# Wide exponentials behind one Silu, value products of two query blocks in one burst, and pre-multiplied last weights in a hybrid transformer block

## The chip, the cores and the metric

The kernel runs on one core of a Trainium2 chip. The metric is the time of one execution on the device in microseconds. In this text TensorE is PE (its weight loads PEld), VectorE is DVE, ScalarE is ACT, GpSimd is POOL, and SyncE, which starts most of the transfers, is SP.

## The reference

One block of a transformer, for one sequence of 1024 tokens of width 1024. A conditioning vector c gives six modulation vectors; attention (8 heads of 64 in three dilated branches) and a gated delta rule (8 heads of 64) run side by side on projections of the normed input; then come an output projection, a SwiGLU network of width 2816 and a last norm:

```python
sh1, sc1, g1, sh2, sc2, g2 = split(silu(c) @ w_ada + b_ada, 6)
h = rmsnorm(x, norm_attn_g) * (1 + sc1) + sh1
q_a, k_a, v_a, q_d, k_d, v_d, z_d, b_d, a_d = split(h @ w_in)
y_attn = dilated_attention(q_a, k_a, v_a, rel_bias)
# delta heads: q, k, v = silu(causal_conv(q_d, k_d, v_d)); q, k = l2norm(q) / 8, l2norm(k)
#   beta = sigmoid(b_d); g = -exp(a_log) * softplus(a_d + dt_bias); gcum = cumsum(g) in a chunk
#   decay[i, j] = exp(gcum[i] - gcum[j]) for j <= i; A = strict_lower((beta k) k^T * decay)
#   u, w = (I + A)^-1 [beta v, beta k exp(gcum)]; then a scan over the chunks carries the state
y_delta = rmsnorm(o, delta_norm_g) * silu(z_d)
x = x + g1 * (concat(y_attn, y_delta) @ w_out)
h = rmsnorm(x, norm_ffn_g) * (1 + sc2) + sh2
x = x + g2 * ((silu(h @ w_gate) * (h @ w_up)) @ w_down)
return rmsnorm(x, final_norm_g)
```

l2norm divides by the square root of the sum of squares plus 1e-6.

## The kernel before, in words

Every large product is made of three matmuls: both operands are split into a high part (a cast, for weights on ACT, line 230, or 1603 in the network) and a low part (a subtraction, on POOL, line 231, or on DVE, line 1604), and high*high, high*low and low*high are added in one PSUM bank. gemm (line 590) and proj_t (line 613) issue them for the projections, down_mm (line 1809) for the last product.

A scheduler orders the instructions of each engine once, when the program is built, by priority and by what they need; each engine then runs its queue in that order and waits at the first instruction whose inputs are not there. Three things steer it: urgent() raises the priority of what is issued within, issue_after(x) puts an instruction behind x, and a table FILL says how many microseconds of projections are put between two pieces of the delta or attention work (ahead, turn).

**The delta heads** are done in two groups g of four heads, as eight blocks n of 128 tokens. conv (lines 549 to 557) is the causal convolution, a scaled copy on ACT, three multiply-adds on DVE (line 553) and a Silu on ACT (line 557). delta_turn transposes a conv's output (line 734, tiles trk and trq), squares it on ACT (line 740) and sums the squares on DVE (line 744) into norms rk (keys) and eq (queries). For group 1 this is done early, by delta_early, which stores the convs' outputs in memory, from where delta(1) loads them again. delta_rows loads the rows of gcum into four tiles dt of 128x1024, one a head, and masks them. delta_prep makes from rk its inverse root by Ln and Exp (lines 761 to 763), subtracts Gc (line 764), and then takes decay * rk as 32 exponentials of 128x128 (line 767), each with its own bias column. kk (line 796) are the products of keys with keys and queries, multiplied with dt on DVE (line 802); the results go to memory (line 809). kt*kds (line 821) and qd*eb (line 836) are on POOL, where eb is one more exponential per pair of heads (line 835) of rows that are loaded just before.

delta_rows_in loads the stored rows again; delta_v (lines 872, 875) makes beta*v; delta_inverse scales by bpr (line 885), runs 31 steps on DVE, each needing the one before (lines 896, 900), writes the result tn to memory and loads it again (lines 903, 905); the products on TensorE that use it begin at line 928. delta_scan carries the state; it takes a power on POOL (line 1063). Meanwhile TensorE does projections as fill, among them va (values of attention) and z. z's output is evacuated by a Silu on ACT (line 634). Silu and Exp lie in different tables of ACT, so a change from one to the other is a table load.

**Attention** takes units of one pair of heads hp and one query block qb of 128 rows, 32 units. att_score (lines 1325 to 1336) makes scores S, adds the bias table and takes the maximum on DVE, the exponential on ACT and the scaling on POOL, into X. att_turn transposes X block by block (line 1349, tiles tr) and copies it to et (line 1354 on ACT for key blocks 0 to 3, line 1352 on DVE for 4 to 7); et has ETB buffers for the two heads of ETB/2 units. att_value multiplies et with va (line 1366), the two heads e side by side in the two halves of the array's columns, in qb+1 steps, into bank y. attend issues the value product of a unit AV = 3 units behind its scores.

**The last product** of the network is a scheme of seven products of half-size matrices, down(0) to down(6); each has 22 slices f of the inner dimension, four row blocks b, and three matmuls each. down_parts loads a slice of both operands and splits them. An "end" of a product adds up what it needs: half_end multiplies by g2 (g2r, line 1858), adds x (xr, line 1859) and squares with a sum (line 1861); row_out takes the root (line 1868), its reciprocal (line 1869), and scales both halves of the row block (line 1874 on ACT, line 1876 on DVE) and stores them. In down(6) the last TAIL = 4 slices are kept back: their matmuls come block by block, with each block's end behind it.

## Time and profile before

| | us |
|---|---|
| median of three runs | 1407.59 (1407.41 to 1409.31) |
| the profiled execution | 1407.41 |
| its span (first to last instruction) | 1405.6 |
| TensorE busy | 1353.3 |
| VectorE, ScalarE, GpSimd busy | 874.6, 660.0, 287.2 |

A row of the profile's groups reads: line, engine, operation, output<-input, shape and count, then the busy time of all, the mean nanoseconds of one, and the idle time of the engine just before them with what ended it. A row of the timeline reads: start, duration, engine, line, operation. A row of waits reads: engine and tile that waited, what it waited for, then the sum in us, how many times, and the longest. In a row of windows each engine's busy time and its instruction count follow the window's length; then come TensorE's granted clock (1.00 is full speed), the DMA share and GB/s. The chain of work that ended last goes back from the last instruction, at each step to what released it.

### The profile page before, as it was taken

What the parts mean: (1) busy time and instruction counts of PE and PEld (TensorE: products, weight loads), DVE (VectorE), ACT (ScalarE), POOL (GpSimd) and SP (SyncE); (2) the same over time, 40 slices, a digit from 0 to 9 for tenths busy, and PEclk for the clock granted to TensorE, in tenths of its full rate; (3) what the DMA queues carried; (4) which work ended last, traced back from release to release, by engine and by line L of the source; (5) the groups of instructions that cost most, each with busy time, mean ns of one, the idle gap of its engine ahead of it and who ended that gap; (6) DMA issues with size and microseconds to landing.
All of it is one profiled execution on the core that took longest, in us unless ns stands there. A gap on an engine that the chain in (4) does not pass through costs nothing.

```text
span 1405.6 us, 24430 instructions
## 1 busy us (share of the span) xinstructions
PE 1353.3 (96%) x8984; PEld 1113.2 (79%) x8984; DVE 874.6 (62%) x1659; ACT 660.0 (47%) x1285; POOL 287.2 (20%) x261
## 2 busy tenths in 40 slices
PE   8998999998999999999999899999999999999997
PEld 4777787888889878777777678888888888888885
DVE  3688573656847242765248987666575776474487
ACT  4497424346233453765168533333333333444456
POOL 2344303324213433543262400000000000000000
PEclk9999999999999999999999999999999999999999
DMA  8666573475362555521675245444453665765566
GB/s 305 225 194 174 173 217 127 135 233 140 120 171 85 173 146 166 158 84 61 198 251 161 97 163 180 157 164 164 137 195 113 209 209 182 255 223 195 195 225 232
DMA packets 169872, 245.65 MB, mean 175 GB/s; under 512 B 32566, under 2 KB 73831, under 8 KB 169752
## 3 DMA queue, kind: packets, MB, share of 16 engines
q1 hardware_dynamic: 169752, 244.08, 54.2%
q8 instruction: 71, 1.16, 0.3%
q14 instruction: 49, 0.40, 0.1%
HBM read 181.27 MB, written 67.48 MB: 177 GB/s over the span
## 4 chain that ended last, share of the span: by engine, by line
PE 71%; DVE 13%; DMA 6%; ACT 4%; issue 3%; POOL 1%; SPq 0%; DVEq 0%; ACTq 0%; POOLq 0%
PE wua L1614 8%; PE wga L1614 8%; PE X L1809 6%; PE g_a L590 4%; PE wuc L1614 4%; PE Z L1809 4%; PE wgc L1614 4%; PE wo L590 3%; PE y L1366 2%; PE Y L1809 2%; PE tr L1349 2%; PE g_va L613 2%; DVE tm L896 2%; PE f L251 2%; PE wgb L1614 2%
## 5 line engine op out<-in xcount | busy, mean ns | idle before, releaser
L1604 DVE TENSOR_TENSOR wl_db<-wr_db,wh_db 128x512 fp32r<-128x512 f32 x77 | 53.2, 690 | 75.7 <-ACT wh_db L1603 75.6
L1603 ACT CAST wh_db<-wr_db 128x512 fp32r<-128x512 f32 x77 | 47.9, 622 | 97.7 <-PE X L1809 41.3
L1329 DVE CUSTOM_DVE_ANT_0 X<-S,ng 128x512 f32<-128x512 f32 (+3 forms) x64 | 36.6, 587 | 61.9 <-PE S L1326 46.4
L1809 PE MATMUL X<-wl_db,wh_da 128*128 128x512 f32 x176 | 68.6, 390 | 0.1
L1336 POOL TENSOR_SCALAR X<-X,sc 128x128 f32<-128x128 f32 (+7 forms) x64 | 50.0, 786 | 91.1 <-DVE sc L1335 77.7
L1809 PE MATMUL X<-wh_db,wl_da 128*128 128x512 f32 x176 | 68.5, 389 | 0.0
L1809 PE MATMUL X<-wh_db,wh_da 128*128 128x512 f32 x176 | 68.5, 389 | 0.0
L1334 ACT ACTIVATE X<-X,sc 128x128 f32<-128x128 f32 (+7 forms) x64 | 49.4, 773 | 33.9 <-DVE sc L1329 31.7
L1604 DVE TENSOR_TENSOR wl_da<-wr_da,wh_da 128x512 fp32r<-128x512 f32 x77 | 52.8, 686 | 1.6 <-ACT wh_da L1603 1.6
L590 PE MATMUL wo<-yh,wh_wo 128*128 128x512 f32 x128 | 51.7, 405 | 1.0 <-DVE xo L1417 1.0
L590 PE MATMUL g_a<-hh,wh_a 128*128 128x512 f32 x128 | 51.8, 404 | 0.0
L590 PE MATMUL wo<-yh,wl_wo 128*128 128x512 f32 x128 | 50.8, 397 | 0.0
L590 PE MATMUL wo<-yl,wh_wo 128*128 128x512 f32 x128 | 50.4, 394 | 0.1
L1603 ACT CAST wh_da<-wr_da 128x512 fp32r<-128x512 f32 x77 | 47.4, 616 | 6.4 <-PE wua L1614 5.9
L590 PE MATMUL g_a<-hl,wh_a 128*128 128x512 f32 x128 | 50.3, 393 | 0.0
L590 PE MATMUL g_a<-hh,wl_a 128*128 128x512 f32 x128 | 50.1, 392 | 0.0
L1603 ACT CAST wh_wg_s<-wg_s 128x512 fp32r<-128x512 f32 x33 | 20.5, 622 | 55.8 <-PE wuc L1614 23.8
L1349 PE MATMUL tr<-ident,X 128*128 128x128 f32 x288 | 42.9, 276 | 1.8 <-ACT et L1354 1.0
L1366 PE MATMUL y<-et,va 128*64 128x128 f32 x576 | 43.9, 280 | 0.0
L231 POOL TENSOR_TENSOR wl_wo<-wr_wo,wh_wo 128x512 fp32r<-128x512 f32 x24 | 32.5, 1357 | 51.7 <-ACT wh_wo L230 51.7
L1603 ACT CAST wh_wg<-wr_wg 128x512 fp32r<-128x512 f32 x31 | 19.3, 621 | 47.2 <-PE wua L1614 19.2
L1603 ACT CAST wh_wu_s<-wu_s 128x512 fp32r<-128x512 f32 x33 | 20.4, 622 | 44.5 <-PE wga L1614 17.5
(545 smaller groups left out, 4349.9 us busy)
## 6 DMA issues: line engine op xcount, KB each, us to landing
wm<-in_wada SPq DMA_DIRECT2D x44, 512.0 KB, 6.0
wr_da<-ao_d SPq DMA_DIRECT2D x77, 256.0 KB, 3.0
wr_wu<-in_wu SPq DMA_DIRECT2D x50, 256.0 KB, 2.8
wr_wg<-in_wg SPq DMA_DIRECT2D x48, 256.0 KB, 3.0
ao_d<-a SPq DMA_DIRECT2D x44, 256.0 KB, 2.6
wr_wd<-in_wdn SPq DMA_DIRECT2D x44, 256.0 KB, 3.0
wr_db<-wt_d SPq DMA_DIRECT2D x44, 256.0 KB, 2.7
ao_d<-as SPq DMA_DIRECT2D x33, 256.0 KB, 2.5
```

Source lines behind the costliest of these rows:

```text
L231: (eng or nc.gpsimd).tensor_tensor(out=lo[:, :n], in0=raw[:, :n], in1=hi[:, :n].bitcast(F32), op=ALU.subtract)
L251: nc.tensor.matmul(first[bank], a[:, w0], b[k][:, cs], start=(k == 0 and n_ == 0), stop=(k == KT - 1 and n_ == 2))
L590: last[0] = nc.tensor.matmul(ps, a[:, w0], b[k0 + k4][:, cs], start=(i == 0), stop=(i == n - 1))
L1329: nc.vector.tensor_tensor_reduce(out=X[:, c0:c1], in0=ps[:, 0 : c1 - c0], in1=ng[:, u + c0 : u + c1], scale=1.0, scalar=(3e38 if m is None ...
L1334: nc.scalar.activation(X[:, 0:nk], X[:, 0:nk], AF.Exp, scale=-1.0, bias=m, accum_out=sc[:, 2:3])
L1336: nc.gpsimd.tensor_scalar(out=X[:, 0:nk], in0=X[:, 0:nk], scalar1=sc[:, 3:4], scalar2=0.0, op0=ALU.mult, op1=ALU.add)
L1349: nc.tensor.transpose(ps[:, (kb - c0) * P : (kb - c0 + 1) * P], X[:, kb * P : kb * P + P], ident)
L1366: nc.tensor.matmul(yps[64 * e : 64 * e + 64, yc], va[:, kb, 64 * e : 64 * e + 64], ets[e][:, kb, :], start=(kb == 0), stop=(kb == qb),)
L1603: nc.scalar.copy(hi, src)
L1604: (eng or nc.vector).tensor_tensor(out=lo, in0=src, in1=hi.bitcast(F32), op=ALU.subtract)
L1614: nc.tensor.matmul(ps, a[:, w0], b, start=(first and k == 0 and n_ == 0), stop=(k == 3 and n_ == 2), skip_group_check=True,)
L1809: nc.tensor.matmul(bank[b], a[:, ts_], w, start=(first and f == 0 and n_ == 0), stop=(f == NF - 1 and n_ == 2), skip_group_check=True,)
```

## The change

It has three parts.

**Group 1 of the delta heads.** delta_rows(1) also subtracts Gc from each dt on DVE, so that the exponential no longer needs a bias per block. delta_exps issues the loads and then six exponentials of 128x1024 (four dt, two eb) one behind the other, the first behind the Silu of the last query conv of delta_early; every later Silu of a conv or of z is put behind the last of them (behind). The inverse root of rk is taken on POOL (add EPS, power -0.5) instead of by Ln and Exp, and delta_prep multiplies dt by rk on DVE, four operations of 128x1024. Group 0 stays as it was.

**Value products.** att_value does two query blocks, an odd one and the one before it, in one urgent burst into one bank; the first three matmuls are put in the order head 1, head 1, head 0, and key blocks are taken from 0 and then downwards (for block 7, from 7 and then upwards). et has six buffers.

**The last product.** The four last slices of down(6) are loaded and split during down(5), with the weights multiplied by g2 beforehand on DVE. Their matmuls go to four banks W of their own, and X*g2 + x is made on DVE while they run, so that a block's end is one addition, the square and the root; the square is scaled so that the other half's sum serves as the root's bias. mhalf grows, and a pad at the end of the constants shrinks to make room.

The diff, cut:

```diff
-XB, ETB, AT, AV = 5, 4, 1, 3
+XB, ETB, AT, AV = 5, 6, 1, 3
...
-    mhalf = const([P, 4], "mhalf")
+    mhalf = const([P, 16], "mhalf")
...
-        nc.scalar.activation(dst, dst, AF.Silu)
+        with tc.issue_after(behind[0].ins) if behind[0] else ExitStack():
+            return nc.scalar.activation(dst, dst, AF.Silu)
...
-            with urgent():
+            with urgent(), tc.issue_after(behind[0].ins) if behind[0] else ExitStack():
                 taken[0] = nc.scalar.activation(zt, ps[:, 0:256], AF.Silu)
...
+            if g:
+                nc.vector.tensor_tensor(
+                    out=dt_, in0=dt_, op=ALU.subtract,
+                    in1=bc(Gc[:, 32 * g : 32 * g + 32].rearrange("p (n h) -> p n h", n=8)[:, :, hl_], P),
+                )
...
+    def delta_exps(last):
+
+        lts = delta_rows(1)
+        ebs = [delta_eb(1, q) for q in range(2)]
+        for t in (*lts, *ebs):
+            with tc.issue_after(last.ins):
+                last = nc.scalar.activation(t, t, AF.Exp)
+        behind[0] = last
+        return lts, ebs
...
+        if norms and kind == "k" and g:
+            v = norms["rk"][:, :, 2 * q : 2 * q + 2]
+            nc.gpsimd.tensor_scalar(out=v, in0=v, scalar1=EPS, scalar2=None, op0=ALU.add)
+            nc.gpsimd.tensor_tensor(
+                out=v, in0=v, in1=mhalf.rearrange("p (n e) -> p n e", e=2), op=ALU.pow,
+            )
...
-        if g == 1:
-            nc.scalar.activation(lr, rk, AF.Ln, bias=eps1)
-        nc.vector.tensor_scalar(out=lr, in0=lr, scalar1=-0.5, scalar2=None, op0=ALU.mult)
-        nc.scalar.activation(rk, lr, AF.Exp)
-        nc.vector.tensor_tensor(out=lr, in0=lr, in1=g3(Gc), op=ALU.subtract)
-        for h in range(4):
-            for n in range(8):
-                nc.scalar.activation(lts[h][:, n], lts[h][:, n], AF.Exp, bias=lr[:, n, h : h + 1])
+        if g == 0:
+            nc.vector.tensor_scalar(out=lr, in0=lr, scalar1=-0.5, scalar2=None, op0=ALU.mult)
+            nc.scalar.activation(rk, lr, AF.Exp)
+            nc.vector.tensor_tensor(out=lr, in0=lr, in1=g3(Gc), op=ALU.subtract)
+            for h in range(4):
+                for n in range(8):
+                    nc.scalar.activation(lts[h][:, n], lts[h][:, n], AF.Exp, bias=lr[:, n, h : h + 1])
+        else:
+            for h in range(4):
+                nc.vector.tensor_tensor(out=lts[h], in0=lts[h], in1=bc(rk[:, :, h], P), op=ALU.mult)
...
-            conv((4 if kind == "k" else 0) + 2 + q, fetch(j, f"{kind}{2 + q}"), t)
+            last = conv((4 if kind == "k" else 0) + 2 + q, fetch(j, f"{kind}{2 + q}"), t)
+            nc.sync.dma_start(_.cv[j], t)
+            if j == 3:
+                made = delta_exps(last)
             delta_turn(1, kind, q, t, norms=norms[1])
-            nc.sync.dma_start(_.cv[j], t)
+        return made
...
     def att_value(hp, qb, ets):
+
         va = loaded[hp][0]
-        if qb % 4 == 0:
+        if qb % 4 == 1:
             ybanks[hp] = ybank(f"y{hp}_{qb}")
         yps = ybanks[hp]
-        yc = slice((qb % 4) * P, (qb % 4 + 1) * P)
-        with turn(f"y{hp}_{qb}"):
-            for kb in range(qb + 1):
-                for e in range(2):
-                    nc.tensor.matmul(
-                        yps[64 * e : 64 * e + 64, yc], va[:, kb, 64 * e : 64 * e + 64], ets[e][:, kb, :],
-                        start=(kb == 0), stop=(kb == qb),
+        seq = {q: (0, *range(q, 0, -1)) if q < 7 else (q, *range(q)) for q in (qb - 1, qb)}
+        parts = [(q, kb, e) for q in (qb, qb - 1) for kb in seq[q] for e in (1, 0)]
+        parts[1:2], parts[2:3] = parts[2:3], parts[1:2]
+        mm = None
+        with turn(f"y{hp}_{qb}"), urgent():
+            for i, (q, kb, e) in enumerate(parts):
+                with tc.issue_after(mm.ins) if i else ExitStack():
+                    ins = nc.tensor.matmul(
+                        yps[64 * e : 64 * e + 64, (q % 4) * P : (q % 4 + 1) * P],
+                        va[:, kb, 64 * e : 64 * e + 64], ets[q % 2][e][:, kb, :],
+                        start=(kb == seq[q][0]), stop=(kb == seq[q][-1]),
                     )
+                mm = ins if i < 2 else mm
...
-            if i >= AV:
+            if i >= AV and units[i - AV][1] % 2:
                 hp, qb = units[i - AV]
-                att_value(hp, qb, ets.pop(i - AV))
+                att_value(hp, qb, [ets.pop(i - AV - 1), ets.pop(i - AV)])
...
+        if p is not None:
+            with urgent():
+                nc.vector.tensor_tensor(out=b, in0=b, in1=g2r[:, dsl[0]], op=ALU.mult)
...
+            if i == 5 and f % 2 == 1 and len(held) < TAIL:
+                t = NF - TAIL + len(held)
+                held[t] = down_parts(6, t, pz)
...
-            if final:
+            if tail:
                 for f in range(n, NF):
-                    down_mm(bank, b, pr[f], f, first)
+                    down_mm(tail, b, held[f], f, f == n, f == NF - 1)
                 with urgent():
-                    final[b]()
+                    last[b]()
...
+        sq = pz.tile([P, HALF], F32, name=f"sq3_{l}{s}{b}", tag="sq3", bufs=2)
+        nc.scalar.activation(sq, t, AF.Square, scale=1.0 / 32, accum_out=rn[:, 4 * l + b, s : s + 1])
...
-        nc.vector.tensor_tensor(out=r[:, 2:3], in0=r[:, 0:1], in1=r[:, 1:2], op=ALU.add)
-        nc.scalar.activation(r[:, 2:3], r[:, 2:3], AF.Sqrt, bias=eps1, scale=1.0 / D)
-        nc.vector.reciprocal(r[:, 3:4], r[:, 2:3])
+        nc.scalar.activation(r[:, 3:4], r[:, 1 - l : 2 - l], AF.Sqrt, bias=r[:, 2:3])
+        nc.vector.reciprocal(r[:, 3:4], r[:, 3:4])
...
+    def last_end(src, more):
+
+        def at(b):
+            x = x_in(1, 0, b)
+            t = y[1, 0][b]
+            nc.vector.tensor_tensor(out=t, in0=src[b], in1=g2r[:, dsl[0]], op=ALU.mult)
+            nc.vector.tensor_tensor(out=t, in0=t, in1=x, op=ALU.add)
+
+            def go():
+                nc.vector.tensor_tensor(out=t, in0=more[b], in1=t, op=ALU.add)
+                square(1, 0, b, t)
+                row_out(1, b)
+
+            return go
+
+        return at
...
-    down(6, X, False, sum_end(1, 0, X, None, True), final=True)
+    W = four("W")
+    down(6, X, False, last_end(X, W), tail=W)
```

In ACT's queue, here from the table load behind the query's Silu on: rk is the inverse norm of keys, sqq the squares of queries, wh_z the high part of z's weights. Before:

```order
L763 ACT_TABLE_LOAD
L763 ACTIVATE rk_1378<-lr_1383 128x32
L1098 COPY va_6_3978<-g_va_6_3953 128x256
L230 CAST wh_z_1_4062<-wr_z_1_4061 128x512
L740 ACTIVATE sqq_0_3490<-trq_0False 128x512
L230 CAST wh_z_2_4068<-wr_z_2_4067 128x512
L767 ACTIVATE dt_0_3536<-dt_0_3536,lr_1383 128x128
```

and, behind more of these narrow exponentials, its end:

```order
L767 ACTIVATE dt_3_3551<-dt_3_3551,lr_1383 128x128 x8
L835 ACTIVATE eb_3817<-eb_3817 128x1024
L835 ACTIVATE eb_3823<-eb_3823 128x1024
L551 ACTIVATE vd_3832<-xp_v_3833,cw 128x1024
L230 CAST wh_z_3_4074<-wr_z_3_4073 128x512
L230 CAST wh_a_0_0_4415<-wr_a_0_0_4414 128x512
```

The same place in the changed kernel:

```order
L553 ACTIVATE vd_3812<-xp_v_3813,cw 128x1024
L560 ACTIVATE cv_3435<-cv_3435 128x1024
L733 ACT_TABLE_LOAD
L733 ACTIVATE dt_0_3444<-dt_0_3444 128x1024
L1132 COPY va_6_3958<-g_va_6_3933 128x256
L230 CAST wh_z_1_4042<-wr_z_1_4041 128x512
L230 CAST wh_z_2_4048<-wr_z_2_4047 128x512
L733 ACTIVATE dt_1_3450<-dt_1_3450 128x1024
L1185 COPY tri<-mods 128x128
L230 CAST wh_z_3_4054<-wr_z_3_4053 128x512
L1132 COPY va_7_4031<-g_va_7_3962 128x256
L733 ACTIVATE dt_2_3456<-dt_2_3456 128x1024
```

The third cast of z's weights stood behind all exponentials and now stands behind the second; a conv's scaled copy (vd) has come ahead of the query's Silu.

In TensorE's queue, the value products of the pair of blocks 4 and 5 near the end of a pair of heads (tr are transposes of X, S scores, wo the output projection as fill). Before, block 5's:

```order
L1349 MATMUL tr_5_4_6798<-ident,X_5_6660 128x128 x2
L1366 MATMUL y_4_6862<-et_5_6780,va_5876 64x128
L1349 MATMUL tr_6_0_6839<-ident,X_6_6754 128x128 x4
L1325 MATMUL S_0_0_6875<-KS_6407,QS_6406 128x128
L1326 MATMUL S_0_0_6875<-KL_6408,QS_6406 128x128
L1349 MATMUL tr_6_4_6845<-ident,X_6_6754 128x128 x3
L1366 MATMUL y_4_6862<-et_5_6791,va_5876 64x128
L1366 MATMUL y_4_6862<-et_5_6780,va_5876 64x128
L1325 MATMUL S_0_0_6884<-KS_6417,QS_6416 128x128
L1326 MATMUL S_0_0_6884<-KL_6418,QS_6416 128x128
L1366 MATMUL y_4_6862<-et_5_6791,va_5876 64x128
L1366 MATMUL y_4_6862<-et_5_6780,va_5876 64x128
```

Now, the start of the burst for both blocks:

```order
L1360 MATMUL S_7_0_6807<-KS_5862,QS_5861 128x512
L1361 MATMUL S_7_0_6807<-KL_5863,QS_5861 128x512
L593 MATMUL wo_1_1_7267<-yl_6691,wh_wo_1_6864 128x512
L593 MATMUL wo_1_1_7267<-yh_6690,wl_wo_1_6864 128x512
L1384 MATMUL tr_6_0_6819<-ident,X_6_6728 128x128 x2
L1405 MATMUL y_5_6898<-et_5_6765,va_5850 64x128 x2
L1405 MATMUL y_5_6898<-et_5_6754,va_5850 64x128 x2
L1405 MATMUL y_5_6898<-et_5_6765,va_5850 64x128
L1405 MATMUL y_5_6898<-et_5_6754,va_5850 64x128
```

The products stood in pieces between transposes and scores; they are one piece now, and two matmuls of one head stand ahead of two of the other.

In DVE's queue of the changed kernel, the end of the program (X and W are the banks of the kept back product, y the output rows):

```order
L1937 TENSOR_TENSOR y_2_12409<-X_12418,g2r 128x512
L1937 TENSOR_TENSOR y_3_12410<-X_12419,g2r 128x512
L1938 TENSOR_TENSOR y_2_12409<-y_2_12409,xr_14380 128x512
L1938 TENSOR_TENSOR y_3_12410<-y_3_12410,xr_14384 128x512
L1941 TENSOR_TENSOR y_0_12407<-W_14156,y_0_12407 128x512
L1920 RECIPROCAL rn<-rn 128x1
L1927 SCALAR_TENSOR_TENSOR y_0_12407<-y_0_12407,rn,gfr 128x512
L1941 TENSOR_TENSOR y_1_12408<-W_14157,y_1_12408 128x512
```

All multiplications and additions of X stand ahead of the first block's end, and a block's addition stands behind the scaling of the block before.

81 lines of the change are left out of this document (43 added, 38 removed).

## The prediction

> **What bounds the kernel now.** I read the page first: how full TensorE is over the span, and which engine carries the chain of work that ended last.
>
> ```profile
> span 1405.6 us, 24430 instructions
> PE 1353.3 (96%) x8984; PEld 1113.2 (79%) x8984; DVE 874.6 (62%) x1659; ACT 660.0 (47%) x1285; POOL 287.2 (20%) x261
> PE 71%; DVE 13%; DMA 6%; ACT 4%; issue 3%; POOL 1%; SPq 0%; DVEq 0%; ACTq 0%; POOLq 0%
> ```
>
> TensorE is busy for 1353.3 of 1405.6 us and holds 71% of the chain. So a part of the change is worth time in two ways only: it takes away a stretch in which TensorE stands (or runs at half clock), or it makes TensorE's own matmuls shorter. The change touches three stages, and I read each by itself: what TensorE waits for there, then the timeline of the engine it waits for.
>
> **Part 1, the second group of delta heads (300 to 395 us).** The waits of TensorE from 300 to 350 us:
>
> ```profile
> PE g_z L613 <- POOL wl_z L231: 3.1, 1, 3.1
> PE trq_0False L734 <- ACT cv L557: 0.7, 1, 0.7
> PE kk_k L796 <- DVE qk L802: 0.5, 2, 0.3
> ```
>
> One wait of 3.1 us stands out: a projection of z stands for the low part of its weights, which POOL makes (line 231) after ACT's cast. ACT's and POOL's timelines show why it is late:
>
> ```profile
> 315.50 1.28 ACT L763 ACT_TABLE_LOAD   x1
> 322.81 8.58 ACT L767 ACTIVATE dt<-dt,lr 128x128 f32<-128x128 f32 x29
> 331.29 2.00 ACT L835 ACTIVATE eb<-eb 128x1024 f32<-128x1024 f32 x2
> 334.23 0.61 ACT L230 CAST wh_z<-wr_z 128x512 fp32r<-128x512 f32 x1
> 334.77 3.39 POOL L836 TENSOR_TENSOR qd<-qd,eb 128x1024 f32<-128x1024 f32 x1
> 338.10 2.25 POOL L231 TENSOR_TENSOR wl_z<-wr_z,wh_z 128x512 fp32r<-128x512 f32 x1
> ```
>
> The cast stands behind 29 narrow exponentials (8.58 us) and two wide ones, and the split on POOL behind qd*eb, which needs the last exponential: 340.35 us until it is done. What follows is dearer than the wait. The windows around it, with the granted clock in the third-last column:
>
> ```profile
> core 0: us, PE busy (x) PEld busy (x) DVE busy (x) ACT busy (x) POOL busy (x), PEclk, DMA share, GB/s
> 340.40:346.05 5.65, 5.64 (x26) 5.64 (x27) 1.03 (x1) 1.33 (x2) 3.23 (x3) 0.50 0.45 115
> 149.77:153.18 3.41, 3.41 (x46) 2.71 (x47) 2.32 (x3) 1.95 (x4) 1.39 (x1) 1.00 0.18 29
> 209.52:212.93 3.41, 3.41 (x19) 3.41 (x18) 0.11 (x1) 1.44 (x3) 2.08 (x2) 0.50 1.08 315
> 300.00:337.00 37.00, 35.69 (x370) 32.14 (x369) 26.61 (x41) 32.84 (x68) 14.67 (x9) 1.00 0.79 219
> ```
>
> After the stall TensorE works for 5.65 us at clock 0.50, which costs 5.65 / 2 = 2.8 us more. The stall is worth 3.1 + 2.8 = 5.9 us.
>
> After the change ACT has the casts of wh_z between the wide exponentials, POOL splits all of z's weights before kt*kds and qd*eb, and TensorE does the last value projection and two z projections before the kk products. The two exponentials of wide form above took 2.00 / 2 = 1.0 us each; six are 6 us where 9.8 us (32 narrow ones) and 2.0 us stood, and of the four table loads of 1.28 us in this stretch two stay. The stall goes. Placed by hand in the new order, small waits are left: 0.4 us more for a query's Silu, which now has a conv copy of 1.1 us ahead of it on ACT, and 0.5 to 1.0 us for the third wl_z. That is 5.9 - 1.2 = 4.7 us up to here, or some 6 us where the two old waits of 0.7 and 0.5 us end too. Who is late next? The inverse chain on DVE, from its last input to its result:
>
> ```profile
> 352.51 1.22 DVE L885 TENSOR_TENSOR nt<-nt,bpr 128x1024 f32<-128x1024 f32 x1
> 355.70 0.18 DVE L896 TENSOR_TENSOR tm<-nt,tt 128x31 f32<-128x31 f32 x1
> 393.45 0.88 DVE L933 STREAM_TRANSPOSE U<-tn 32x256 f32<-32x256 f32 x2 [8.59 <-DMA tn<-tn_d]
> ```
>
> and TensorE's only wait from 384 to 395 us:
>
> ```profile
> PE lv L928 <- DMA tn<-tn_d: 0.7, 1, 0.7
> ```
>
> It starts at 355.70, is a serial chain on DVE and then a trip through memory, and TensorE already waits 0.7 us for its result at 393.4. So TensorE cannot gain more there than the chain does. In the new order the chain's first step follows a conv, the transposes of v and nt*bpr, all of which move ahead with TensorE: I place it at 350.7, 5.0 us earlier. **I take 5.0 us**, with bounds 2.0 (the chain held by DVE's added work) and 6.5 (all that the stall and its small companions cost).
>
> The covers: DVE gets eight more operations of 128x1024 with two inputs, nearest row nt*bpr with 1.22 us, together 9.8 us. DVE has 37.0 - 26.6 = 10.4 us free from 300 to 337 us (last window row). Four subtractions come before the exponentials, beside the convs; the four multiplications by rk stand ahead of the products with kk, which now come later. If that cover is gone, up to half of them, 4.9 us, falls on the chain; that is the lower bound. The norm's power on POOL has a near row, the scan's, with four elements a partition (a group of sixteen):
>
> ```profile
> L1063 POOL TENSOR_TENSOR of<-of,mhalf 128x4 f32<-128x4 f32 x16 | 16.3, 1016 | 21.1 <-DVE of L1060 20.3 <-PE g_va L613 0.7
> ```
>
> For 16 elements I bound it by 1.0 us (a fixed cost) and 4.1 us (four times as much), and take 2. Two of them and two additions stand beside the convs and the last value projections, and POOL is idle for 37.0 - 14.7 = 22.3 us from 300 to 337 us; nothing on the path.
>
> At one place a rule of the Trainium skill speaks here. The page "TensorE: Matmul & The Clock Gate", Part 1, lets the clock fall to half only after an idle window of about 3.4 us; by it a stall of 3.1 us would not have to cost its 2.8 us of slow clock, and a gain without these would be 2.2 us and the time 1396.8 us. The row at 340.40 shows half clock right behind 3.1 us, and the one at 209.52 behind 1.9 us; the measurement decides, the sum keeps the 2.8 us, and no chance is kept for the rule here.
>
> **Part 2, the value products of attention (486 to 663 us).** Here TensorE hardly waits; what the change moves is its own time. All 576 records in one group, then TensorE's timeline around one burst, and one long burst:
>
> ```profile
> L1366 PE MATMUL y<-et,va 128*64 128x128 f32 x576 | 43.9, 280 | 0.0
> 510.84 0.71 PE L1349 MATMUL tr<-ident,X 128*128 128x128 f32 x5
> 511.48 1.09 PE L1366 MATMUL y<-et,va 128*64 128x128 f32 x16
> 512.50 0.50 PE L590 MATMUL g_a<-hh,wh_a 128*128 128x512 f32 x1
> 512.83 0.40 PE L590 MATMUL g_a<-hl,wh_a 128*128 128x512 f32 x1
> 513.07 0.40 PE L590 MATMUL g_a<-hh,wl_a 128*128 128x512 f32 x1
> 546.36 1.97 PE L1366 MATMUL y<-et,va 128*64 128x128 f32 x32
> 548.26 0.50 PE L590 MATMUL g_a<-hh,wh_a 128*128 128x512 f32 x1
> ```
>
> A matmul has two records, and two heads go side by side, so 16 records are four pairs. From start to start the burst of four pairs takes 1.02 us and that of eight 1.90: 0.218 us a pair and 0.15 us a burst. Each burst costs its neighbours too. The five transposes before it take 0.64 us to its start, four steps of 0.109 and a last one of 0.203, so 0.09 late; the wide matmul behind it takes 0.33 instead of 0.24, so another 0.1 (0.06 where a transpose follows; 0.08 on the mean). In the timeline I count 47 bursts in all; their starts to the next work add up to 41.8 us, more than 47 x 0.15 + 144 x 0.218 = 38.4 because a pair that is cut in two costs twice.
>
> After the change there are 16 bursts of 3, 7, 11 and 15 pairs, four times each: 16 x 0.15 + 144 x 0.218 = 33.8 us. Their order is new, e1 e1 e0 e0 at the start and then alternating. A matmul of one half whose partner stands one place later starts later; the bound is one pair more a burst (0.33 with its wait) and nothing. I take 0.22 (one pair's time), 3.5 us in all: 37.3. The gain is 41.8 - 37.3 = 4.5, and 31 fewer bursts x (0.09 + 0.08) = 5.3, together 9.8 us.
>
> A sentence of the Trainium skill bears on it. "TensorEngine Tiling (Array Packing)", Key Properties, charges a drain for a change of the tiling mode and none for a change of tile; by that the swap at the start is free and the time 1390.5 us, which stands below as a rival; the rows agree on the cost at a burst's edges, and none shows a swap.
>
> Against this stands TensorE's queue, which runs in order. A whole burst now needs the copies et of two query blocks, and these copies (ACT line 1354, DVE line 1352) wait for buffers and for each other. The windows of the stage's fuller half:
>
> ```profile
> 570.00:615.00 45.00, 44.11 (x335) 33.09 (x335) 34.51 (x106) 34.81 (x73) 22.82 (x23) 1.00 0.49 136
> 615.00:665.00 50.00, 48.41 (x437) 39.16 (x436) 30.50 (x91) 29.39 (x65) 19.48 (x21) 1.00 0.22 75
> ```
>
> and from the waits of TensorE and of ACT from 486 to 665 us the rows on et:
>
> ```profile
> PE tr L1349 <- ACT et L1354: 1.0, 2, 0.8
> ACT et L1354 <- PE y L1366: 13.5, 13, 2.5
> ```
>
> DVE and ACT are busy for 77% of the fullest stretch, TensorE waits there for little. The wait of et copies for value products shows that buffers do run out; with six instead of four, every second unit finds them free. In the new order a few bursts stand less than 1 us behind the transposes that feed them. I charge 1.5 us. **Part 2 gives 9.8 - 1.5 = 8.3 us**, bounds 4 (waits of 0.4 us at each of 16 bursts) and 12 (no swap, no waits).
>
> **Part 3, the end (1365 us on).**
>
> The last matmul and the last row's end in the timeline:
>
> ```profile
> 1396.18 0.39 PE L1809 MATMUL X<-wh_db,wl_da 128*128 128x512 f32 x1
> 1400.53 0.28 ACT L1868 ACTIVATE rn<-rn,eps 128x1 f32<-128x1 f32 x1
> 1401.04 0.75 DVE L1876 SCALAR_TENSOR_TENSOR y<-y,rn,gfr 128x512 f32<-128x512 f32 x1
> ```
>
> and two links of the chain that ended last:
>
> ```profile
> 1396.97 0.61 DVE y L1859
> 1397.67 0.73 ACT sq L1861 x2
> ```
>
> TensorE ends at 1396.57 (T) and the last row is scaled at 1401.79, T + 5.2; the rest is the way out. After the change the eight operations that add x to X*g2 ahead (0.6 us each, by the add in the chain) can start only when X is complete, 48 matmuls of 0.227 us before T, T - 10.9, and DVE's queue has them all ahead of the first block's end. So this starts at T - 5.6 at the earliest. DVE's queue then takes a block at a time: add, wait for square and root, reciprocal, scale. From these rows a block takes 0.70 (an add's start to the square's), 0.73, 0.51 (the root's start to the scaling's) and 0.75, together 2.7 us, and four end at T - 5.6 + 4 x 2.7 = T + 5.3. That is where it was: **0**, bounds -1.5 (DVE later by two or three operations) and +2.5 (TensorE the bound: T + 2.7 is one block's time). The multiplications of W by g2 add four operations to DVE in the stage before and the earlier splits fill it, but TensorE keeps two f in hand.
>
> **The sum.** 5.0 + 8.3 + 0 = 13.3 us off the profiled execution's 1407.41 us (span 1405.6 and 1.8 around it): 1394.1, and the median of three runs is 0.18 higher than that execution, so 1394 us. All lower bounds give 2.0 + 4 - 1.5 = 4.5 us, 1403; all upper ones 21, 1386.
>
> **Rivals.**
> - *The paired products' gain is eaten by waits for et.* For it: 77% of DVE and ACT, buffers that run out, and a queue that cannot go around a waiting burst. Against: AV = 3 units lie between, and TensorE waits 1.0 us for ACT's et in the row above. Part 2 then gives at most 3 us: about 1399.
> - *The delta gain is given back at tn.* For it: the chain of 31 steps is fixed and TensorE waits for it already; if DVE's added products hold its start, only 1 us is left: about 1398. Against: its inputs come from TensorE's products, which move ahead.
> - *The swap is free:* each half of the array goes on when its own last product is done. Part 2 gains 3.5 us more: 1390.5. Against: nothing in this trace shows two orders of the same burst.
> - *It does not do what it says*: the small waits add up to the old ones, and the bursts are as dear as the fragments: 1407, within 0.2%.
> - *Slower, by one mechanism:* a pair's burst waits about 2 us for an et copy, and TensorE's clock halves behind it, as in the row at 209.52 (3.41 us at 0.50, 1.7 us lost): 3.7 us a time. The clock did not fall at 149.77 after a wait as long. From (13.3 + 2.8) / 3.7 = 4.4, so five of 16 such bursts, it is slower than before by over 0.2%; six give 1416 us.
>
> **Chances.** The forecast 0.40, a free swap 0.10, waits for et 0.19, tn 0.12, no effect 0.07, slower 0.12. Differences under 0.2% (2.8 us) can't be told from none here. Faster by more than that: the first four, 0.81, less 0.01 for their upper ends; same 0.08; slower 0.12. The range goes from 1386, all upper bounds, to 1405, which takes in the first four; what is left out is no effect and slower, 0.19.
>
> **What would show it.** In the changed profile: no wait of g_z for wl_z, and clock 1.00 from 335 to 350 us (part 1 right); an lv that still waits for tn (the chain as its limit), by 0.5 to 2 us. The value products as 16 bursts, the longest of 15 pairs about 3.4 us or up to 3.7; waits of y for et under 2 us in sum. The last row scaled 5 to 5.5 us behind the last matmul. I am wrong if TensorE waits over 5 us for et between 486 and 660, if windows behind a burst show clock 0.50, or if DVE's multiplications by rk stand between the kk products and their results.

## The result, and the profile after

The changed kernel takes a median of 1413.06 us (1410.63 to 1415.48, seven runs) against 1407.22 us (1404.39 to 1409.31, seven runs) of the kernel before: a ratio of 1.0043 (95% interval 1.0027 to 1.0058). It is slower by 0.4%, where 1394.0 us was forecast. Here and below, a few executions more than 1.5% above the fastest of their kernel are left out of the ratios. The profiled execution took 1410.63 us. Its page:

```profile
span 1408.9 us, 24366 instructions
PE 1348.8 (96%) x8984; PEld 1111.0 (79%) x8984; DVE 889.4 (63%) x1673; ACT 651.0 (46%) x1253; POOL 301.9 (21%) x265
```

TensorE's matmuls became 4.5 us shorter (1353.3 to 1348.8), and the span 3.3 us longer: TensorE stands 7.8 us more. To see where, I compare the starts of the same matmuls in both traces. Two tiles serve as marks. yt is the transposition of the delta heads' output: its first start lies in group 0's scan, its last at the end of group 1's. x2t is the transposition behind attention. In the view of a tile, the three times behind the count are ns (least, median, most), and then come its first and last start. Before:

```profile
L1075 PE MATMUL yt<-ident,o x32: 271/273/421, 262.4 to 458.8; 128*128 128x128 f32 x32
L1476 PE MATMUL x2t<-ident,x x64: 270/272/327, 705.5 to 760.8; 128*128 128x128 f32 x64
```

After:

```profile
L1109 PE MATMUL yt<-ident,o x32: 270/273/330, 264.0 to 465.4; 128*128 128x128 f32 x32
L1516 PE MATMUL x2t<-ident,x x64: 270/272/329, 707.3 to 764.3; 128*128 128x128 f32 x64
```

So the changed kernel is 6.6 us behind at the end of the delta heads (465.4 - 458.8), has made up 4.8 us by the end of attention (1.8 behind at 705), and ends 3.3 us behind. Part 1 lost, part 2 gained.

**Part 1's stretch.** The waits of TensorE from 300 to 420 us after the change:

```profile
PE g_z L616 <- ACT zt L637: 4.6, 1, 4.6
PE g_z L616 <- POOL wl_z L231: 2.9, 3, 1.3
PE g_va L616 <- ACT sp_a L1142: 1.3, 1, 1.3
PE kk_q L835 <- DMA qd<-cv_d: 1.2, 1, 1.2
PE kk_q L835 <- ACT kt L773: 0.4, 1, 0.4
```

and the windows between 250 and 420 us in which the granted clock is 0.50:

```profile
core 0: us, PE busy (x) PEld busy (x) DVE busy (x) ACT busy (x) POOL busy (x), PEclk, DMA share, GB/s
257.14:263.96 6.82, 6.82 (x32) 6.53 (x31) 3.05 (x12) 0.91 (x3) 1.65 (x2) 0.50 0.09 31
325.41:328.82 3.41, 3.33 (x15) 3.33 (x16) 2.87 (x3) 0.00 (x0) 2.25 (x2) 0.50 0.51 146
335.65:342.47 6.82, 6.78 (x57) 6.79 (x59) 3.40 (x6) 0.94 (x1) 4.28 (x2) 0.50 0.02 4
362.96:366.37 3.41, 3.41 (x19) 3.41 (x18) 3.13 (x9) 0.00 (x0) 0.00 (x0) 0.50 0.39 123
```

The one wait of 3.1 us for wl_z is gone, as one wait; three shorter ones of 2.9 us in sum are left. In all there are now waits of 10.4 us, and behind them slow clock in the last three windows that costs (3.33 + 6.78 + 3.41) x 0.50 = 6.8 us. Before, the same stretch had 6.0 us of waits and 2.8 us of slow clock. The dearest of the new waits, 4.6 us for a Silu of z on ACT, is a wait for a store to memory, as ACT's row with its releaser and SP's queue show:

```profile
362.15 0.73 ACT L637 ACTIVATE zt<-g_z 128x256 f32<-128x256 f32 x2 [7.36 <-DMA va_d<-va]
343.23 8.96 SPq L848 DMA_DIRECT2D lt_d<-dt  x16
355.10 0.47 SPq L1134 DMA_DIRECT2D va_d<-va  x1
355.61 7.27 SPq L639 DMA_DIRECT2D zg_d<-zt  x4
```

ACT idles 7.36 us for the store of va that frees a buffer. That store stands in SP's queue behind sixteen stores of the key products' results, which wait for these products: the change moved projections ahead of the products, and their outputs fill four buffers before SP comes to them.

The first loss lies where the prediction did not look, at 252 us. DVE's timeline there after the change:

```profile
252.85 2.28 DVE L720 TENSOR_TENSOR dt<-dt,Gc 128x1024 f32<-128x1024 f32 x1 [5.83 <-POOL dt L715]
255.14 0.95 DVE L1062 COPY S<-st 64x64 f32<-64x64 f32 x4
```

The first of the new subtractions is queued ahead of the copy of group 0's state. DVE idles 5.83 us until POOL's mask is there, the subtraction takes 2.28, and the copy stands behind it. TensorE waits 3.4 us for that copy in the changed kernel (first row); at the same place the kernel before waits 1.4 us for the state's update (second row):

```profile
PE st L1029 <- DVE S L1062: 3.4, 1, 3.4
PE st L995 <- DVE S L1030: 1.4, 1, 1.4
```

The changed kernel then runs 6.82 us at clock 0.50 (first window above), which costs another 3.4 us; in the trace of before half as much, 1.7 us, is lost behind the 1.4.

**Part 2's stretch.** All value products, one burst of 15 pairs with its neighbour, and the waits of TensorE on them and on the transposes and scores from 486 to 670 us:

```profile
L1405 PE MATMUL y<-et,va 128*64 128x128 f32 x576 | 35.1, 275 | 0.3 <-ACT et L1389 0.2
540.04 3.50 PE L1405 MATMUL y<-et,va 128*64 128x128 f32 x60
543.48 0.50 PE L593 MATMUL g_a<-hl,wh_a 128*128 128x512 f32 x1
PE S L1360 <- DVE sc L1364: 2.7, 6, 1.0
PE tr L1384 <- ACT et L1389: 1.7, 3, 1.0
PE tr L1384 <- DVE et L1387: 1.0, 1, 1.0
PE tr L1384 <- POOL X L1371: 0.9, 3, 0.4
PE y L1405 <- ACT et L1389: 0.2, 1, 0.2
```

The products hardly wait (0.2 us); the transposes and scores behind them do. A burst of 15 pairs takes 3.44 us from its start to the next work.

**Part 3's stretch.** The last matmul, the last addition and the last scaling:

```profile
1401.45 0.39 PE L1854 MATMUL W<-wh_db,wl_da 128*128 128x512 f32 x1
1401.87 0.69 DVE L1941 TENSOR_TENSOR y<-W,y 128x512 f32<-128x512 f32 x1
1403.88 0.75 DVE L1927 SCALAR_TENSOR_TENSOR y<-y,rn,gfr 128x512 f32<-128x512 f32 x1
```

TensorE ends at T = 1401.84, the last scaling at 1404.63, T + 2.8, where before it was T + 5.2.

### The profile page after: what moved, and what is told of

Same layout as the page of the kernel before. It is cut to its first block, busy times and chain, and to the rows that moved or that the text cites. A ratio compares the mean times of both kernels' runs of the same rounds, so it can differ in the third digit from the quotient of the medians.

```text
span 1408.9 us, 24366 instructions
## 1 busy us (share of the span) xinstructions
PE 1348.8 (96%) x8984; PEld 1111.0 (79%) x8984; DVE 889.4 (63%) x1673; ACT 651.0 (46%) x1253; POOL 301.9 (21%) x265
## 4 chain that ended last, share of the span: by engine, by line
PE 73%; DVE 12%; DMA 6%; ACT 4%; issue 3%; POOL 2%; SPq 0%; DVEq 0%; ACTq 0%; POOLq 0%
PE wua L1654 8%; PE wga L1654 8%; PE X L1854 6%; PE g_a L593 5%; PE wo L593 5%; PE wuc L1654 4%; PE wgc L1654 4%; PE Z L1854 3%; PE Y L1854 2%; PE y L1405 2%; PE g_va L616 2%; PE wgb L1654 2%; PE wub L1654 2%; PE f L251 2%; PE tr L1384 2%
## 5 line engine op out<-in xcount | busy, mean ns | idle before, releaser
L1854 PE MATMUL X<-wl_db,wh_da 128*128 128x512 f32 x160 | 62.4, 390 | 0.3 <-DVE wl_db L1644 0.3
L1854 PE MATMUL X<-wh_db,wh_da 128*128 128x512 f32 x160 | 62.3, 389 | 0.0
L1854 PE MATMUL X<-wh_db,wl_da 128*128 128x512 f32 x160 | 62.3, 389 | 0.0
L1384 PEld LDWEIGHTS tr<-ident,X 128*128 128x128 f32 x288 | 32.7, 140 | 15.1 <-POOL X L1371 5.2
L616 PE MATMUL g_z<-wh_z,hh 128*128 128x256 f32 x128 | 38.1, 298 | 6.0 <-ACT zt L637 6.0
```

The costliest lines, as they stand in the source:

```text
L616: last[0] = nc.tensor.matmul(ps[:, :n], a[k][:, ts_], b[:, w0], start=(i == 0), stop=(i == 23))
L1384: nc.tensor.transpose(ps[:, (kb - c0) * P : (kb - c0 + 1) * P], X[:, kb * P : kb * P + P], ident)
L1854: nc.tensor.matmul(bank[b], a[:, ts_], w, start=(first and n_ == 0), stop=(last and n_ == 2), skip_group_check=True,)
```

## The experiments

The theories at first were T1 (part 1's loss comes from DVE's added multiplications, which slow POOL's splits and hold the products' results) and T2 (it comes from the new order of TensorE's work, which makes the key products late and fills buffers). Later ones came in as these fell; each expectation names its own.

The table has all kernels with the ratio of their runs to the kernel before. The other columns are from one trace each, in us: the first yt, the time from first to last yt (most of the delta heads) and from last yt to first x2t (attention), read from the two rows of tiles as shown above. Two more take the time from first to last yt apart: W is the sum of TensorE's waits in it, and S is what slow clock costs there, half of the time that TensorE works at clock 0.50.

| kernel | ratio (95%) | first yt | first to last yt | of it W | of it S | to x2t |
|---|---|---|---|---|---|---|
| before | 1 | 262.4 | 196.4 | 10.2 | 3.7 | 246.7 |
| after | 1.0043 (1.0027 to 1.0058) | 264.0 | 201.4 | 13.6 | 6.8 | 241.9 |
| e1_delta | 1.0066 (1.0052 to 1.0080) | 267.8 | 201.6 | 15.2 | 5.0 | 246.7 |
| e2_values | 0.9963 (0.9940 to 0.9987) | 261.0 | 194.8 | 9.5 | 2.9 | 242.5 |
| e3_last | 0.9996 (0.9982 to 1.0011) | 260.4 | 194.3 | 10.0 | 1.6 | 247.3 |
| e4_values_last | 0.9961 (0.9941 to 0.9982) | 258.8 | 195.2 | 10.9 | 1.4 | 242.1 |
| e6_no_rk | 1.0073 (1.0053 to 1.0094) | 267.8 | 198.3 | 13.0 | 4.7 | 245.8 |
| e8_exps_later | 1.0080 (1.0058 to 1.0102) | 266.1 | 205.5 | 14.1 | 11.8 | 246.8 |
| e9_all_exps_later | 1.0039 (1.0013 to 1.0065) | 263.9 | 205.8 | 12.8 | 13.5 | 242.0 |
| e10_sub_late | 1.0039 (1.0019 to 1.0058) | 258.9 | 204.5 | 15.5 | 7.4 | 246.3 |
| e12_sub_late_no_rk | 1.0070 (1.0044 to 1.0096) | 261.5 | 204.5 | 16.7 | 5.3 | 247.9 |
| e13_qeb_late | 1.0008 (0.9984 to 1.0032) | 260.0 | 194.4 | 10.4 | 1.7 | 250.4 |
| e14_best | 0.9968 (0.9940 to 0.9996) | 261.7 | 193.9 | 9.9 | 1.7 | 242.4 |
| e15_later_none | 1.0001 (0.9980 to 1.0022) | 257.9 | 197.2 | 12.9 | 1.7 | 247.7 |
| e16_later_sub_late | 1.0069 (1.0046 to 1.0092) | 260.0 | 201.5 | 12.8 | 6.0 | 247.6 |
| e17_none (trace of e17b_none) | 1.0022 (1.0000 to 1.0044) | 261.0 | 200.7 | 13.5 | 6.7 | 246.8 |
| e18_no_sub | 1.0047 (1.0028 to 1.0065) | 260.8 | 200.3 | 15.6 | 2.9 | 247.2 |
| e19_pool_sub | 1.0117 (1.0092 to 1.0142) | 264.7 | 210.1 | 19.5 | 10.7 | 245.5 |
| e20_no_qeb | 0.9999 (0.9972 to 1.0026) | 262.5 | 191.8 | 8.4 | 0.7 | 248.6 |

Before, e2, e3 and e4 run the same code for the delta heads. Their first yt lies between 258.8 and 262.4 and their time from first to last yt between 194.3 and 196.4: that is how far one trace can be trusted. Without W and S, the time from first to last yt is between 179 and 183 us in every row: the kernels differ there by waits of TensorE and by slow clock, and by little else.

### The parts alone

One part each of the change, the rest as before; e4 has parts 2 and 3. Part 1 alone, for one, takes back from the changed kernel:

```diff
-XB, ETB, AT, AV = 5, 6, 1, 3
+XB, ETB, AT, AV = 5, 4, 1, 3
...
-            if i >= AV and units[i - AV][1] % 2:
+            if i >= AV:
...
-    down(6, X, False, last_end(X, W), tail=W)
+    down(6, X, False, sum_end(1, 0, X, None, True), final=True)
```

> Part 1 alone (the second group of delta heads as in the change, everything else as before). Theory A, the loss is in part 1: by the landmarks of the changed kernel's trace TensorE loses 7.0 us between 299 and 420 us (0.4 us early there, 6.6 us late here), so this kernel takes about 1407.2 + 7 = 1414 us, with TensorE waiting for wl_z by about 2.9 us and for zt by about 4.6 us. Rival B, the loss is made elsewhere and the delay of part 1 is only shifted work that later stages would have waited for anyway: within 2.8 us of 1407.2.

> Part 2 alone (paired value products, six et buffers). Theory A: the attention stage gains 4.7 us from 465 to 705 us (6.6 us late becomes 1.9 us late in the changed kernel), so about 1402.5 us, and up to 1.7 us more or less by where the slow clock falls afterwards. Rival B, the paired bursts are what costs time (waits for et and slow clock behind them): 1409 us or more.

> Part 3 alone (modulated last weights, own banks for the last slices). Theory A: the last matmul ends 1.9 us later and the tail behind it is 2.0 us shorter, so no change, 1406 to 1408.5 us. Rival C, the late matmuls (1.6 us lost in down(5)) come only from the other parts' shift and not from part 3's own DVE load: 1405 us.

> Parts 2 and 3 without part 1. Theory A, the parts add up: about 1402.5 us, faster than before by 0.3%. Rival B: no faster than before, 1406 us or more, as part 2 gains only what part 1's delay had left idle.

Part 1 alone loses 0.66% (9.3 us of 1407.2), part 2 alone gains 0.37% (5.2 us), part 3 alone does nothing that can be measured. Their sum, +0.25%, agrees with the whole change within the intervals. e4 beats both kernels: a median of 1402.13 us. e1's trace shows the same waits as after, with the zt, qd and wl_z rows at

```profile
PE g_z L616 <- ACT zt L637: 4.4, 1, 4.4
PE kk_q L835 <- DMA qd<-cv_d: 3.0, 1, 3.0
PE g_z L616 <- POOL wl_z L231: 2.8, 3, 1.3
```

### Part 1: the multiplications, or the order?

e6 is part 1 without the multiplications by rk; e8 is part 1 with the six exponentials issued in delta(1), behind the copies of the keys, so that the key products come early again; e9 is the whole change with that edit.

```diff
 e6
-            for h in range(4):
-                nc.vector.tensor_tensor(out=lts[h], in0=lts[h], in1=bc(rk[:, :, h], P), op=ALU.mult)
 e8, e9
-            if j == 3:
-                made = delta_exps(last)
-        return made
+        return last
-        delta_prep(g, st, norms[g], kt[0:2], *(made or (delta_rows(g), None)))
+        delta_prep(g, st, norms[g], kt[0:2], *(delta_exps(made) if g else (delta_rows(g), None)))
```

> Part 1 alone without the four DVE multiplications of dt by rk (this part of the computation is left out; TensorE's order is that of part 1 alone). Theory T1, all of the loss starts at POOL: its three splits of wl_z run beside these multiplications and take 2.6 us each instead of 1.3, and the waits of z, the late loads of qd behind SP's blocked queue and the late kk products follow from it. Then the splits take 1.3 us each, no wait for wl_z is left and the time falls from 1416.3 to 1408 us or less. Theory T2, the order is the cause: the exponentials stand ahead of the query's squares and the key copies on ACT, so TensorE's kk products come behind 48 z matmuls and some 10 us later, and all behind them too. Then only the wl_z waits go (2.8 us and up to 1.7 us of slow clock), the wait for zt of 4.4 us stays, and the time is 1411 to 1414 us.

> Part 1 alone, with the six exponentials issued behind delta(1)'s key copies in the program instead of ahead of the last query's squares; they still follow that query's Silu in one table set, with all multiplications by rk. In the order kk comes ahead of most of z again. Theory T2: the gain that the change was forecast to bring appears, no wait for zt, 1402 to 1405 us. Theory T1: POOL's splits still run beside the multiplications, z still waits for wl_z, and the time is 1411 us or more.

> The whole change with the exponentials issued later, as in the run before it. Theory T2: parts 1 and 2 both gain, 1397 to 1401 us, the fastest so far. Theory T1: 1408 us or more.

In e6, POOL's splits do speed up, as its row shows, three in 4.52 us where after (first row) has 7.74:

```profile
317.69 7.74 POOL L231 TENSOR_TENSOR wl_z<-wr_z,wh_z 128x512 fp32r<-128x512 f32 x3 [3.49 <-PE mods L211]
322.45 4.52 POOL L231 TENSOR_TENSOR wl_z<-wr_z,wh_z 128x512 fp32r<-128x512 f32 x3 [3.79 <-PE mods L211]
```

TensorE's wait for wl_z falls to 0.2 us, but 4.1 us for zt and 3.5 us for qd remain, and the time is no shorter (1.0073): T1 falls as the whole cause. In e8 TensorE waits instead for DVE, whose queue has the multiplications ahead of the products' results:

```profile
PE kk_k L835 <- DVE qk L841: 3.9, 1, 3.9
PE kk_q L835 <- DMA qd<-cv_d: 1.6, 1, 1.6
```

The zt wait falls to 0.5 us, and the time is as long as before that edit or longer: T2 falls as the whole cause too. e9, the whole change with that edit, stays at 1.0039 where after has 1.0043. e8 and e9 have the largest S of the table, for in both traces TensorE runs at clock 0.50 for 17.1 us from 402 and 400 us on, behind waits of 2.0 and 2.2 us; no other trace has this. Whoever takes one wait away meets the next; the two costs lie beside each other.

### The added work on DVE

e10 is part 1 with the four subtractions behind the last multiply-add of the last query conv on DVE; e12 has that and no multiplications; e16 is e10 with the exponentials of e8. e18 has no subtractions, e17 neither subtractions nor multiplications, e15 neither, with the exponentials of e8. e19 has the subtractions on POOL. e17b is e17 again, one execution, and the trace is from it.

```diff
 e10, e12, e16 (removed from delta_rows)
+        for h in range(4):
+            with tc.issue_after(stt[0].ins):
+                nc.vector.tensor_tensor(
+                    out=lts[h], in0=lts[h], op=ALU.subtract,
 e15, e17, e18 (e15 and e17 without the multiplications by rk as well)
-            if g:
-                nc.vector.tensor_tensor(
-                    out=dt_, in0=dt_, op=ALU.subtract,
 e19
-                nc.vector.tensor_tensor(
+                nc.gpsimd.tensor_tensor(
```

> Part 1 alone, with the four subtractions of Gc put behind the last query conv's last multiply-add on DVE. Theory M1: in the changed kernel the first of them stands in DVE's queue ahead of group 0's state copy, waits for POOL's mask of dt, and TensorE waits 3.4 us for that copy, with slow clock behind it; by the landmarks of part 1 alone that is 5.7 us between 254 and 262 us. Then that wait goes and the time falls from 1416.3 to 1408 to 1412 us. Rival: the subtractions now hold the exponentials and the multiplications behind them, the loss moves to 310 to 350 us, and the time stays at 1414 us or more.

> The same with the four multiplications by rk left out (this part of the computation is left out). Theory: the loss of part 1 has its causes one behind the other, the subtraction ahead of the scan (5.7 us), POOL's splits beside the multiplications (some 3 us) and the order on ACT (2 us); then 1407 to 1410 us, with the waits for qd and for zt still there. Rival: the late kk products are all of it and cost 7 us by themselves: 1413 us or more.

> All the work of part 1, exponentials behind the key copies and subtractions behind the last query conv. Theory O: 1404 to 1408 us. Theory D: 1411 us or more, since the eight operations stand in DVE's queue ahead of the kk products (TensorE's kk_k waited 3.9 us for them in the run with the exponentials later).

> The same eight operations left out, and the exponentials behind the key copies. Theories D, O and B agree that it is near the kernel before or faster, 1401 to 1408 us, as both suspects are gone; if it is still 1412 us or more, the cause is a third one, the norms on POOL, the Silus held behind the exponentials or the queue of loads.

> Part 1 alone without the four subtractions of Gc and without the four multiplications by rk (left out), exponentials at the change's place on ACT. Theory D, DVE's added work is the cause: near the kernel before, 1404 to 1409 us. Theory O, the order on ACT is the cause (squares and key copies behind the exponentials, kk late, waits for qd and zt): 1412 us or more. Theory B, both: in between or no better than theory O.

> Part 1 alone without the eight operations, one look at its trace. If the order on ACT alone cost time, the waits of kk_q for qd and of g_z for zt stand here as in part 1 alone (3 and 4.4 us); if they were a consequence of DVE's and POOL's load, they are shorter than 1 us each.

> Part 1 alone without the four subtractions of Gc (left out); the multiplications by rk are there. Theory S, the subtractions are the dear half, because the first of them stands in DVE's queue ahead of group 0's state copy and TensorE waits 3.4 us there: ratio 1.001 to 1.004, 1408 to 1412 us, no wait of st for S over 2 us. Rival, it takes all eight to load DVE, and each half alone is enough for most of the loss: 1.006 or more.

> Part 1 alone with the subtractions on POOL behind its masks, all work done. Theory S: DVE's queue no longer holds the state copy, 1408 to 1412 us. Rival, POOL's longer chain of mask, subtraction and power moves the norms and all behind them later: 1414 us or more.

The early subtraction is shown by the column of the first yt. In all six traces that have it where the change put it, on DVE or POOL, it lies between 263.9 and 267.8 (mean 265.7); in the six with the subtractions late or gone between 257.9 and 261.5 (mean 260.0), and in the seven with the delta code's DVE work as before between 258.8 and 262.5. That is a loss of some 5 us. Between 240 and 270 us TensorE waits 3.3 to 3.8 us for the state in the first six and 1.5 to 2.3 us in the next six, and slow clock costs 2.5 to 4.8 us against 0 to 1.7. Late subtractions cost less in sum (e10 1.0039 against 1.0066), but not nothing: the time from first to last yt grows to 204.5.

All eight operations out, part 1 still does not gain: 1.0022 with the exponentials at the change's place, 1.0001 with them later. So DVE's work costs some 0.44% (1.0066 to 1.0022, 6 us). How it divides is open: no subtractions 1.0047, no multiplications 1.0073, and late subtractions without multiplications 1.0070, which was expected below 1.0039. These do not add, and the waits show one reason: a wait for nbp, read below, stands with 3.0 to 4.2 us in all seven traces of part 1 with the subtractions late, gone or on POOL, and in none of the five with an early subtraction on DVE (after, e1, e6, e8, e9). Taking the early subtraction away uncovers it. Why e12 is slower than e10, with less work, stays open. Of the expectations, e10's time held (1411.99 us); e12, e18 and e19 came out above the time of the theory that they tested (1415.48, 1414.24 and 1423.86 us). The wait for zt belongs to the order on ACT: it is 3.6 to 5.0 us in all eight traces with the exponentials at the change's place and at most 1.0 us in the four with them later.

POOL is a worse place for the subtractions (1.0117). There the first one stands ahead of the square of group 0's outputs on POOL, the state's update on DVE stands behind the sum of these squares, and TensorE waits 3.7 us for the state all the same; later it waits 3.1 us for the queries' conv.

What is left in e15 is mainly one wait in place of the stall, behind the norms' power on POOL:

```profile
PE ps_bp L808 <- DVE nbp L802: 4.2, 1, 4.2
PE kk_k L827 <- DVE qk L833: 1.8, 2, 1.4
```

nbp needs rk, and POOL's two powers of 128x16 take 3.77 and 2.94 us there. In e17b the same wait is 3.0 us, with 3.6 for zt and 2.0 for qd. No run takes the power off POOL, so what this wait costs in time is not shown.

### Is the stall worth its price?

The rival: the stall of 3.1 us hid another wait, so that it is worth little by itself. e13 is the kernel before, with POOL's qd*eb put behind the split of z's last weights; e14 is e4 with that edit. e20 is the kernel before without qd*eb for group 1.

```diff
 e13, e14
-            nc.gpsimd.tensor_tensor(
-                out=qd[hp], in0=qd[hp], in1=eb.rearrange("p n i -> p (n i)"), op=ALU.mult
-            )
+            late_eb.append((hp, eb))
...
+        if g == 1:
+            delta_qeb(splits["z1_3"])
 e20
+            if g == 0:
+                nc.gpsimd.tensor_tensor(
```

> The kernel before with one order edge: POOL's qd*eb stand behind the split of z's last weights (narrow exponentials, everything else as before). That takes away the wait of 3.1 us and nothing else. Theory P, the price of the prediction holds (3.1 us and 2.8 us of slow clock, the inverse chain moves ahead with it): 1401 to 1403 us. Rival Q, the inverse chain's result is the limit and TensorE only waits later: 1405 us or more.

> Parts 2 and 3 of the change with that one order edge in place of part 1. Theory P: 1396 to 1399 us, faster than before and after. Rival Q: 1401 us or more.

> The kernel before without POOL's two products qd*eb of group 1 (left out), order otherwise the same. If POOL's products slow v's conv on DVE and that is why the stall could not be had, the two multiply-adds take 2.6 us instead of 5.69, no wait for v's Silu over 1 us takes the place of the 3.1 us for wl_z, and the time is 1401 to 1403.5 us. If v's conv is late anyhow, TensorE waits for it as long as before and the time is 1405 us or more.

e13's time is the old one (1.0008), and the trace says why. Its largest waits from 300 to 420 us, and the window behind the first:

```profile
PE trv L884 <- ACT vd L559: 3.0, 1, 3.0
PE lv L940 <- DMA tn<-tn_d: 1.3, 1, 1.3
341.00:344.50 3.50, 3.50 (x21) 3.50 (x20) 2.98 (x4) 1.15 (x1) 1.53 (x3) 0.59 0.35 51
```

No wait for wl_z, but 3.0 us for v's conv a few microseconds later, and slow clock behind that one. The wait for tn, rival Q's limit, grows only from 0.7 to 1.3 us: Q has the time right (e13's median is 1409.39 us) and not the reason. ACT's row of v's conv (vd, at 339.29) waits for DVE:

```profile
333.51 5.69 DVE L555 SCALAR_TENSOR_TENSOR vd<-xp_v,cw,vd 128x1022 f32<-128x1022 f32 x2
339.29 1.06 ACT L559 ACTIVATE vd<-vd 128x1024 f32<-128x1024 f32 x1 [4.33 <-DVE vd L555]
```

Two multiply-adds take 5.69 us while POOL works on qd*eb and a split. In e20, without qd*eb, the same two:

```profile
336.63 3.69 DVE L553 SCALAR_TENSOR_TENSOR vd<-xp_v,cw,vd 128x1022 f32<-128x1022 f32 x2
```

and the wait is 1.2 us. The time from first to last yt is 194.4 in e13 and 193.9 in e14 against 194.3 to 196.4 of unchanged code, and the waits in it sum to 10.4 and 9.9 us against 9.5 to 10.9: the stall, worth 5.9 us by the prediction, brings 1 us at most when it is taken away alone. e14 is not better than e4. e20's time from first to last yt is shorter (191.8), but its runs tell no gain (0.9999); one trace does not settle whether the rest was given back.

## Why the prediction was wrong, step by step

**"The stall goes" and "Who is late next? The inverse chain on DVE"**: this step failed. The wait of 3.1 us went, but who is late next is not the inverse chain; it is v's conv in the same place (e13: 3.0 us) when only the stall goes, and zt, qd or nbp (up to 5.0, 3.7 and 4.2 us) when part 1 does it. The prediction placed the chain's first step at 350.7 us, 5.0 earlier than before; in after it stands at 358.88, 3.2 later. TensorE does not wait for tn there at all, so the rival that gives the gain back at tn did not happen either. Part 1 was forecast at +5.0 us, with bounds 2.0 and 6.5; alone it measured -9.3 us. (The upper bound is also not the sum of the rows that it names: 3.1 + 2.8 + 0.7 + 0.5 = 7.1.)

The price of the stall was too high as well. Its 2.8 us of slow clock were one execution's: the kernel before and e3, both behind the same wait of 3.1 us, have

```profile
339.23:346.05 6.82, 5.64 (x26) 5.64 (x27) 2.17 (x2) 1.33 (x2) 4.40 (x4) 0.50 0.37 96
```

and

```profile
336.93:340.34 3.41, 3.15 (x14) 3.15 (x15) 1.29 (x1) 1.33 (x2) 3.35 (x4) 0.50 0.29 82
```

That is 5.64 x 0.50 = 2.8 us in before and 3.15 x 0.50 = 1.6 us in e3. That the clock can fall behind a wait of this length is borne out (0.59 in e13 behind 3.0 us); the rule of the Trainium skill that the prediction weighed beside it ("TensorE: Matmul & The Clock Gate", Part 1), by which it would not, gave no better number for the stage.

**"The covers"**: failed. The prediction summed DVE's free time from 300 to 337 us, 10.4 us against 9.8 us of new work, and bounded a lost cover at 4.9 us. The first subtraction stands at 252.85, outside that window, and costs through what is queued behind it, the state's copy, not through its own length. All eight cost some 6 us. "Nothing on the path" for the norm's power failed too: it takes 3.77 and 2.94 us, taken as 2, and where the early subtraction is gone TensorE waits 3.0 to 4.2 us for nbp behind it.

**Part 2**: the mechanism was right, the size was off. The bursts are 16 and go as 0.157 + 0.218 us a pair (3.43 us for 15 pairs, 0.81 for 3): their sum fell from 41.8 us, of which 1.0 was waiting behind them, to 34.0. So the swap is free, as the rule of the Trainium skill cited in the prediction ("TensorEngine Tiling (Array Packing)", Key Properties) has it, and the 3.5 us for it were the first mis-sized term. The transposes gained 3.7 us, where 31 x 0.09 = 2.8 were forecast for their late ends. But the stage as a whole gained 5 us: the column to x2t has 241.9 to 242.5 in the five traces with part 2 (mean 242.2) and a mean of 247.2 in the fourteen without.

Between the marks of before and after, counted from start to start, value products and transposes fell by 6.9 + 3.7 us, the wide matmuls between them (g_a, wo) grew by 3.3, the scores by 0.4, and waits by 2.4 (5.3 to 7.7). The largest mis-sized term is therefore the wide matmuls: with 0.08 us less at each of 31 bursts they were to fall by 2.5 us. One reason is in the order: 34 of them stand right behind a transpose where 16 did, at about 0.09 us more each. The waits were charged at 1.5 us, for et; TensorE waits for S's scaling and for X besides. So 8.3 became 5 us. No clock fell behind a burst in after; the rival that ends slower was not that. The bounds were narrower than their own terms (9.8 - 16 x 0.4 = 3.4 and 9.8 + 3.5 = 13.3, given as 4 and 12).

**Part 3**: 0 was forecast and measured (0.9996), but by two errors that cancel, so this hit is luck. The last row is done 2.4 us sooner behind the last matmul, the end that the prediction gave as "TensorE the bound". A block's 2.7 us held; the start of the first one was the mis-sized term: its addition stands at 1393.79, T - 8.1 and not T - 5.6, for the first multiplication of X starts at 1388.90, while TensorE still works on X. Against this, TensorE comes to its last matmul 1.9 us later than its lag at 1276 us (3.4) accounts for (1401.84 - 1396.57 = 5.3). Of this, 1.6 us is lost in down(5), where DVE has the multiplied weights to make: from 1347 to 1363 us matmuls that read wl_db, the split's low part, start up to 0.35 us late.

**The rival that ended slower** has the outcome, slower by over 0.2%, but not the place: it put its waits with slow clock behind them at et, and they stand in the delta heads. What would have shown it before: the order of DVE's queue with the new subtractions, and the rows beside them.

## What to carry to other kernels

An engine's free time in a window covers nothing by itself: in a queue that runs in order, look up at which row each added operation stands, what it waits for there, and who waits for what is behind it. Before a stall is priced, look for the next wait at the same place, for a stall often hides one as long; the cheapest test takes away only the stall, as e13 did here. Take the slow clock behind a wait as a range, not as one price. Of a change with several parts, measure each alone: here 0.37% was gained by one and 0.66% lost by another.
